# Moving the matmul operands of a one-core trunk kernel to fixed places modulo 512 bytes

## The chip, the cores and the metric

The kernel runs on one core of a Trainium2 chip. The metric is the device time in microseconds (us) of one execution, the median of three runs. The engines are called PE (TensorE, the matmul engine; PEld is its loading of weights), DVE (VectorE), ACT (ScalarE), POOL (GpSimd) and SP (SyncE, which here issues DMAs). A matmul holds one operand in the array, the stationary one, and streams the other through it, the moving one; the next stationary operand is loaded while the present moving one streams.

## The reference, cut to what matters

One layer for 256 tokens of 2048 features: `h = rmsnorm(x)`, then `proj = h @ w_in` (2048 features to 18,448 columns), which is cut into the inputs of three branches. A gated convolution of 31 taps with a layernorm, ending in `@ w_conv_out`; a gated linear attention of four heads with decays, ending in `@ w_gla_out`; a cross attention of four heads into 256 memory tokens, `rmsnorm(mem) @ w_mem_kv`, ending in `@ w_mem_out`. Three sigmoid gates weigh the branches, and `x + y @ w_out` is normalized at the end. All in float32. Nearly all the arithmetic is in the products of the 256 tokens with the weight matrices.

## The kernel before, in words

**Products.** Each float32 operand is split in two parts of 12 significant bits, `hi` and `lo`, and each product is three matmuls (`mm3`, lines 158 to 160): hi by hi, hi by lo, lo by hi. Work is done in groups of 512 output columns and 2048 input features, which are 16 tiles of 128. There are two kinds of groups:

- `group_t` puts output features on partitions. Stationary are 128 columns of the weights, moving are the 256 tokens of the activations: 16 tiles x 4 x 3 = 192 matmuls of 256 columns. There are 19 such groups, called by their output tiles: ca0 to ca3 and cb0 to cb3 (convolution), q0, q1, k0, k1, mk, mq, mz, and cz0 to cz3.
- `group_n` puts tokens on partitions. Stationary are 128 tokens, moving are the 512 columns of the weights: 16 tiles x 2 x 3 = 96 matmuls of 512 columns. On the normalized x (tiles `xh` and `xl`) these are v1 to v3, gm0 to gm3, gz0 to gz3, go0 to go3 and gc0 to gc3, 19 in all, and va and vb with 264 columns. On other operands these are mv, yo, yc, out and the short ym.

**Weights.** `chunk` streams two tiles of 128 features at a time from HBM by a DMA on SP's queue into `raw` (4 buffers), ACT copies them to `hi` (line 140) and DVE subtracts to `lo` (line 141), 5 buffers each. These three have a higher priority in the scheduler, so that they run ahead of their use.

**Side work.** Norms, taps of the convolution (`conv_taps`, 480 instructions on DVE, line 359), the scores of the linear attention and the rest are generators that `tick` advances between the chunks; their small matmuls go between those of a group. Their tiles come from rings: `t2` (2048 bytes a partition, 8 buffers), `t1`, `u`, and `b4` (4096 bytes, 19 buffers). The scheduler lays the order of each engine down when the kernel is built.

**Places in SBUF.** Tiles follow each other in a partition in the order in which they are asked for, each padded to 32 bytes. In the program of the kernel before, `xh` and `xl` start at 384 modulo 512 bytes, and `raw`, `hi`, `lo` and all `b4` tiles at 448. Within a tile, 128 columns are 512 bytes, 256 are 1024 and 512 are 2048. So in the groups on `xh` and `xl` weights lie 64 bytes after x modulo 512, and in the groups whose activations are `b4` tiles they lie at the same place. The latter are ca0, cb0, q0, k0 (x not yet normalized), mk and mv (memory), ym, yo, yc and out. In va and vb the second tile of a chunk lies another 32 bytes later, since 264 columns are 1056 bytes.

Of the kernel before, what the change touches and what calls it, by code (L numbers as in the profile page):

```python
# [16 lines left out]
P = 128  # L17
# [16 lines left out]
NB4, NB2, NB1, NRAW, NHL = 19, 8, 8, 4, 5  # L34
NU, LAG, HELD, XWAIT = 2, 2, 12, 4
SPARE = 1.2
AHEAD = 400
# [12 lines left out]
# columns of the packed per-feature vectors  # L50
# [5 lines left out]
def trunk_kernel(ctx, tc, streamed, xt, memt, x, weights, w_alpha2, vecs, taps, b_gate, b_conv_out,  # L56
# [26 lines left out]
    # ---- side work: generators that are advanced between the chunks of weights. They yield how much  # L83
    # work they gave the vector engine, or ("wait", n) to go on n chunks later. ----
# [5 lines left out]
    def start(gen, rank=1):  # L90
        """Tasks of a lower rank go first."""
        task = [gen, 0, rank]
        at = len(Side.queue)
        while at and Side.queue[at - 1][2] > rank:
            at -= 1
        Side.queue.insert(at, task)
        return task
# [28 lines left out]
    def chunk(w, k, a, cols, name, spare=False):  # L126
        """Rows of a tiles of 128 features from tile k on, cols: (first, count) side by side. The weights
        lie in memory in the order in which they are asked for."""
        b = sum(n for _, n in cols)
        at = sum(P * a * sum(n for _, n in cols) for _, _, a, cols in streamed)  # L130
        streamed.append((w, k, a, cols))
        raw = wp.tile([P, a, b], F32, name=f"raw_{name}", tag="raw", bufs=NRAW)
        if spare:
            hi, lo = b4([P, a, b], f"hi_{name}", F32R), b4([P, a, b], f"lo_{name}", F32R)
        else:
            hi = wp.tile([P, a, b], F32R, name=f"hi_{name}", tag="hi", bufs=NHL)
            lo = wp.tile([P, a, b], F32R, name=f"lo_{name}", tag="lo", bufs=NHL)
        with tc.high_priority(offset=AHEAD):
            nc.sync.dma_start(raw, weights[at:at + P * a * b].rearrange("(p k c) -> p k c", p=P, k=a))
            nc.scalar.copy(hi, raw)  # L140
            nc.vector.tensor_sub(lo, raw, hi.bitcast(F32))  # L141
        return hi, lo

    def chunks(w, cols, nk, acts, name, first=CK, spare=False):
        if not isinstance(cols, list):
            cols = [(cols, GC)]
        k = 0
        while k < nk:
            ck = min(CK, first) if k < 2 * first else CK
            hi, lo = chunk(w, k, ck, cols, f"{name}_{k}", spare and k + ck > nk - HELD and k < nk - 8)  # L150
            ops = [acts(k + kk) for kk in range(ck)]
            for kk in range(ck):
                yield k + kk, hi[:, kk, :], lo[:, kk, :], *ops[kk]
            k += ck
            tick()
# [6 lines left out]
    def group_t(w, c0, acts, nk, name, first=CK):  # L162
        """Output features on partitions: two tiles of [128, 2, tokens]."""
        pss = [mm_tile(f"pt_{name}_{j}") for j in range(2)]
        for k, hi, lo, ah, al in chunks(w, c0, nk, acts, name, first):
            for n in range(4):
                cols = slice(n * P, (n + 1) * P)
                mm3(pss[n // 2][:, (n % 2) * T:(n % 2 + 1) * T], hi[:, cols], lo[:, cols], ah, al,
                    k == 0 and n % 2 == 0, k == nk - 1)
        return [p.rearrange("p (a b) -> p a b", a=2) for p in pss]  # L170

    def group_n(w, c0, acts, nk, name):
        """Tokens on partitions: one tile of [128, 512], or of the columns, per token tile."""
# [28 lines left out]
    def token_bcast(col, r, name):  # L202
        """[tokens, 1] per token tile -> r, [128, tokens], the same row on each partition."""
# [8 lines left out]
    def feat_sum(src, name):  # L212
        """Sum over partitions of [128, tokens] -> PSUM [tokens, 1] per token tile."""
# [6 lines left out]
    def square_sum(part, src, name, squared=False):  # L220
        """part (or None) + the sum of squares over the 4 feature tiles of src."""
# [19 lines left out]
    tap = const.tile([P, KT, TAPS], F32, name="tap")  # L241
    mhalf = const.tile([P, 2], F32, name="mhalf")
    nc.gpsimd.memset(mhalf, -0.5)
    reset = const.tile([P, 2 * T], F32, name="reset")
    nc.gpsimd.memset(reset, 1.0)
    nc.gpsimd.memset(reset[:, 0:2 * T:CHUNK], 0.0)
    msk = const.tile([P, len(LEVELS), P], U8, name="msk")

# [1 line left out]
    def raw_operand(src, v0, name, keep):  # L250
        """Loads and splits as it is asked for: the operands, the loaded tiles or their squares."""
# [36 lines left out]
    mrb = const.tile([P, T], F32, name="mrb")  # L288
# [40 lines left out]
    def conv_group(g, acts, rb=None):  # L329
        pa = group_t("w_in", C_A + g * GC, acts, KT, f"ca{g}", CK if rb is None else 1)  # L330
        if g == 0:
            load_constants()
        pb = group_t("w_in", C_B + g * GC, acts, KT, f"cb{g}")
# [14 lines left out]
        return start(conv_taps(g, u), rank=2)  # L348

    def conv_taps(g, u):  # L350
        cg = b4([P, 4, T], f"conv{g}")
        conv.append(cg)
        for i in range(4):
            c = 4 * g + i
            acc = cg[:, i, :]
            nc.vector.tensor_scalar(acc, u[:, i, 0:T], tap[:, c, 0:1], vec[:, V_DB + c:V_DB + c + 1],
                                    op0=ALU.mult, op1=ALU.add)
            for j in range(1, TAPS):
                nc.vector.scalar_tensor_tensor(acc, u[:, i, j:j + T], tap[:, c, j:j + 1], acc,  # L359
                                               op0=ALU.mult, op1=ALU.add)  # L360
                yield 0.4
# [37 lines left out]
    def silu_psum(pz, name):  # L399
        """silu of a PSUM tile."""  # L400
# [8 lines left out]
    cum = []  # L409

    def decay(alr):
        """alr: per token tile the low-rank inputs, in columns 0 and 64 on the upper, 32 on the lower bits."""
# [16 lines left out]
        for i in range(2):  # L429
# [13 lines left out]
            # log_sigmoid(z) = min(z, 0) - ln(1 + exp(-|z|)); sums inside chunks of TAU * log_a  # L443
# [7 lines left out]
            for j in range(2):  # L451
                nc.vector.tensor_tensor_scan(cm[:, 2 * j:2 * j + 2, :].rearrange("p a b -> p (a b)"), reset,
                                             zb[:, 2 * j * T:2 * (j + 1) * T], 0.0, ALU.mult, ALU.add)
# [3 lines left out]
    def load_constants():  # L457
        nc.sync.dma_start(idents, ident_in)
        nc.sync.dma_start(tap, taps)
# [9 lines left out]
    def gla_head(h, q, k, v):  # L469
        """q, k: [128, 2, tokens] of the head, q scaled; v: per token tile [128, 512]."""  # L470
# [5 lines left out]
        # Scores are made as [key, query] for the two token tiles at once. The second tile has its keys  # L476
        # in reverse order, so that in each block its lower half lies where the first has its upper one.
# [13 lines left out]
        # the diagonal, where nothing decays, and pairs of neighbours, where only the query does  # L491
# [33 lines left out]
        # key in the lower and query in the upper half of a block of 2 L tokens: both decays  # L525
        # are taken to the end of the lower half, so that no exponent is positive
# [23 lines left out]
        # key in the first, query in the second half of the sequence  # L550
# [30 lines left out]
        # o = scores @ v, and its rmsnorm  # L581
# [36 lines left out]
    def v_group(h, q, k):  # L618
# [5 lines left out]
        else:  # L624
            # together with the low-rank inputs of the decays
# [98 lines left out]
    def gated_gla():  # L724
        """The normalized o times silu(z), transposed, times the gain of the norm, split."""
# [139 lines left out]
    fss = const.tile([P, NT, 4], F32, name="fss")  # L865
    def residual(po, n, t):
        """Adds x; the mean of the squares goes to fss, the gain of the final norm to res."""
# [12 lines left out]
    fs3 = const.tile([P, NT], F32, name="fs3")  # L880
# [21 lines left out]
    # the last columns: the second token tile ends HELD feature tiles after the first  # L902
# [60 lines left out]
```

## Time and profile before

| | |
|---|---|
| time, median of 3 runs | 1247.44 us (1246.75 to 1247.57) |
| span of the profiled execution | 1246.8 us |
| mean granted clock of TensorE | 0.999 |
| busy: PE, PEld, DVE, ACT, POOL | 1231.0, 1093.9, 964.0, 591.8, 18.6 us |
| instructions: PE, DVE, ACT | 7338, 1502, 711 |
| read from HBM | 235.06 MB, 190 GB/s over the span |

The profiled execution has no time of its own beside its span; the span is 0.6 us under the median of the runs and within their range. Busy is the time in which an engine has an instruction at work. Matmuls overlap, and their ends are modelled, so a matmul's own length says little; what the stream costs is read from the distance between the starts of consecutive matmuls.

### The profile page before, as it was taken

To read this page: it belongs to the slowest core of one execution; us is meant where nothing else is said; L and a number is where in the kernel's file an instruction comes from. 1 tells how busy PE (TensorE), PEld (TensorE's weight loads), DVE (VectorE), ACT (ScalarE), POOL (GpSimd) and SP (SyncE) were. 2 spreads that over 40 slices of the span, in tenths; PEclk is the share of its full clock that TensorE was granted. 3 is DMA by queue.
4 is the path that set the end of the run, shared out by engine and by line. 5 is a ranking of instruction groups with operands and counts; after the bars stand their busy time and mean duration, and the time that the engine had idled before them with its cause. 6 is when DMAs were issued, how large, how long until landed. Compare 5 with 4: busy or idle time off the path is not lost.

```text
span 1246.8 us, 18825 instructions
## 1 busy us (share of the span) xinstructions
PE 1231.0 (99%) x7338; PEld 1093.9 (88%) x7338; DVE 964.0 (77%) x1502; ACT 591.8 (47%) x711; POOL 18.6 (1%) x29
## 2 busy tenths in 40 slices
PE   7999999999999999999999999999999999999997
PEld 7999899988998998889988888888999888888885
DVE  7999999699999667999699979964565554655553
ACT  7534676446553454444445445544354444444442
POOL 0000000000020000000000000000000000000000
PEclk9999999999999999999999999999999999999999
DMA  7565745446545445665465555565555655567562
GB/s 272 186 191 170 236 153 195 155 161 221 188 165 193 159 152 183 205 204 193 161 218 171 200 201 171 179 228 194 195 183 190 202 202 195 205 227 268 187 215 71
DMA packets 71672, 238.37 MB, mean 191 GB/s; under 512 B 7792, under 2 KB 12144, under 8 KB 71584
## 3 DMA queue, kind: packets, MB, share of 16 engines
q1 hardware_dynamic: 71440, 237.13, 56.6%
q8 instruction: 57, 0.93, 0.3%
q14 instruction: 31, 0.25, 0.1%
q10 hardware_dynamic: 144, 0.05, 0.0%
HBM read 235.06 MB, written 2.10 MB: 190 GB/s over the span
## 4 chain that ended last, share of the span: by engine, by line
PE 97%; DMA 1%; DVE 1%; issue 0%; SPq 0%; ACT 0%; POOLq 0%; DVEq 0%; POOL 0%
PE pt_cb L158 2%; PE pt_cz L158 2%; PE pt_cb L159 2%; PE pt_cb L160 2%; PE pt_cz L159 2%; PE pt_cz L160 2%; PE pn_gc L159 2%; PE pn_gm L159 2%; PE pn_gz L158 2%; PE pn_go L159 2%; PE pn_go L158 2%; PE pn_gm L158 2%; PE pn_gz L159 2%; PE pn_yo L158 2%; PE pn_go L160 2%; PE pn_gc L160 2%
## 5 line engine op out<-in xcount | busy, mean ns | idle before, releaser
L359 DVE SCALAR_TENSOR_TENSOR conv<-u,tap,conv 128x256 f32<-128x256 f32 x480 | 207.3, 474 | 0.0
L158 PE MATMUL pt_ca<-xh,hi_ca 128*128 128x256 f32 x256 | 72.7, 289 | 6.1 <-ACT xh L187 5.1
L159 PE MATMUL pt_ca<-xl,hi_ca 128*128 128x256 f32 x256 | 73.5, 288 | 0.2
L160 PE MATMUL pt_ca<-xh,lo_ca 128*128 128x256 f32 x256 | 72.7, 287 | 0.9 <-DVE lo_ca L141 0.9
L158 PE MATMUL pt_cb<-xh,hi_cb 128*128 128x256 f32 x256 | 72.4, 283 | 0.0
L141 DVE TENSOR_TENSOR lo_yc<-raw_yc,hi_yc 128x1024 fp32r<-128x1024 f32 x32 | 39.2, 1225 | 42.9 <-ACT hi_yc L140 42.9
L160 PE MATMUL pt_cz<-xh,lo_cz 128*128 128x256 f32 x256 | 71.9, 281 | 0.0
L158 PE MATMUL pt_cz<-xh,hi_cz 128*128 128x256 f32 x256 | 71.9, 281 | 0.0
L159 PE MATMUL pt_cz<-xl,hi_cz 128*128 128x256 f32 x256 | 71.9, 281 | 0.0
L160 PE MATMUL pt_cb<-xh,lo_cb 128*128 128x256 f32 x256 | 71.8, 282 | 0.0
L159 PE MATMUL pt_cb<-xl,hi_cb 128*128 128x256 f32 x256 | 71.8, 281 | 0.0
L141 DVE TENSOR_TENSOR lo_cz<-raw_cz,hi_cz 128x1024 fp32r<-128x1024 f32 x32 | 39.2, 1224 | 35.7 <-ACT hi_cz L140 35.7
L141 DVE TENSOR_TENSOR lo_gc<-raw_gc,hi_gc 128x1024 fp32r<-128x1024 f32 x32 | 39.1, 1223 | 34.2 <-ACT hi_gc L140 34.2
L141 DVE TENSOR_TENSOR lo_out<-raw_out,hi_out 128x1024 fp32r<-128x1024 f32 x32 | 39.0, 1224 | 31.5 <-ACT hi_out L140 31.2
L140 ACT CAST hi_gc<-raw_gc 128x1024 fp32r<-128x1024 f32 x32 | 33.6, 1052 | 50.3 <-PE pn_yc L160 24.9
L140 ACT CAST hi_yc<-raw_yc 128x1024 fp32r<-128x1024 f32 x32 | 33.7, 1053 | 49.5 <-PE pn_gc L160 33.4
L140 ACT CAST hi_yo<-raw_yo 128x1024 fp32r<-128x1024 f32 x32 | 33.6, 1051 | 46.7 <-PE pn_go L160 23.4
L141 DVE TENSOR_TENSOR lo_yo<-raw_yo,hi_yo 128x1024 fp32r<-128x1024 f32 x32 | 38.8, 1221 | 21.6 <-ACT hi_yo L140 21.6
L158 PEld LDWEIGHTS pt_ca<-xh,hi_ca 128*128 128x128 f32 x256 | 49.5, 196 | 6.4 <-ACT xh L187 5.1
L140 ACT CAST hi_gm<-raw_gm 128x1024 fp32r<-128x1024 f32 x32 | 33.6, 1050 | 45.2 <-PE pn_gm L160 24.6
L140 ACT CAST hi_go<-raw_go 128x1024 fp32r<-128x1024 f32 x32 | 33.7, 1052 | 44.6 <-PE pn_yo L160 24.6
L140 ACT CAST hi_cz<-raw_cz 128x1024 fp32r<-128x1024 f32 x32 | 33.6, 1050 | 44.3 <-PE pt_cz L159 36.0
(352 smaller groups left out, 4108.9 us busy)
## 6 DMA issues: line engine op xcount, KB each, us to landing
raw_cb<-in_weights SPq DMA_DIRECT2D x32, 512.0 KB, 3.5
raw_gm<-in_weights SPq DMA_DIRECT2D x32, 512.0 KB, 3.2
raw_gz<-in_weights SPq DMA_DIRECT2D x32, 512.0 KB, 3.3
raw_go<-in_weights SPq DMA_DIRECT2D x32, 512.0 KB, 3.6
raw_yo<-in_weights SPq DMA_DIRECT2D x32, 512.0 KB, 3.2
raw_cz<-in_weights SPq DMA_DIRECT2D x32, 512.0 KB, 3.2
raw_gc<-in_weights SPq DMA_DIRECT2D x32, 512.0 KB, 3.2
raw_yc<-in_weights SPq DMA_DIRECT2D x32, 512.0 KB, 3.2
```

What stands on the lines that cost most here:

```text
L140: nc.scalar.copy(hi, raw)
L141: nc.vector.tensor_sub(lo, raw, hi.bitcast(F32))
L158: nc.tensor.matmul(o, lhsT=ah, rhs=bh, start=first, stop=False, skip_group_check=True)
L159: nc.tensor.matmul(o, lhsT=ah, rhs=bl, start=False, stop=False, skip_group_check=True)
L160: nc.tensor.matmul(o, lhsT=al, rhs=bh, start=False, stop=last, skip_group_check=True)
L359: nc.vector.scalar_tensor_tensor(acc, u[:, i, j:j + T], tap[:, c, j:j + 1], acc, op0=ALU.mult, op1=ALU.add)
```

## The change

- Constants are rearranged: `tap` (1984 bytes a partition) goes; each convolution group loads its own 496 bytes into a ring of two, by a DMA on SP's queue between its two products. `reset` is half as long, so that the scan of `decay` is 8 instructions of 256 columns in place of 4 of 512. `fss` and `fs3` are made earlier. `mrb` is the same tile as `xrb`. `t2` has 7 buffers.
- By the sizes of the tiles, `xh` then starts at 23424 - 1984 - 1024 + 64 = 20480 bytes, which is 0 modulo 512, and `raw`, `hi`, `lo` and `b4` start at 0 too. `hi` and `lo` tiles are 4608 bytes, nine times 512.
- For `group_t` alone the view of the weights starts 64 bytes into `hi` and `lo` (LINE is 16 elements), and in chunks 0 and 4 of a group (KICK) the second tile starts at 128 modulo 512. In ca0, whose first two chunks hold one tile each, these are tiles 0, 1 and 9, in all others tiles 1 and 9. Activations lie at 0.
- For `group_n` weights and activations lie at 0, also in va and vb, whose second tile now starts 2048 bytes after the first.

Comments are taken out; nothing else of the order in which the program is written changes.

```diff
-NB4, NB2, NB1, NRAW, NHL = 19, 8, 8, 4, 5
+NB4, NB2, NB1, NRAW, NHL = 19, 7, 8, 4, 5
+LINE, HLW = 16, CK * GC + P
+KICK = (0, 4)
...
+    def parts(a, b, name, spare, at):
+        both = []
+        for part in ("hi", "lo"):
+            if spare:
+                t = b4([P, a, b], f"{part}_{name}", F32R)
+                both.append([t, [t[:, j, :] for j in range(a)]])
+                continue
+            t = wp.tile([P, HLW], F32R, name=f"{part}_{name}", tag=part, bufs=NHL)
+            step, first = GC, 0
+            if at:
+                first = LINE * at[0]
+                step = GC + LINE * (at[-1] - at[0])
+            v = t[:, first:first + a * step].rearrange("p (k c) -> p k c", k=a)[:, :, 0:b]
+            both.append([v, [v[:, j, :] for j in range(a)]])
+        return both
...
-        if spare:
-            hi, lo = b4([P, a, b], f"hi_{name}", F32R), b4([P, a, b], f"lo_{name}", F32R)
-        else:
-            hi = wp.tile([P, a, b], F32R, name=f"hi_{name}", tag="hi", bufs=NHL)
-            lo = wp.tile([P, a, b], F32R, name=f"lo_{name}", tag="lo", bufs=NHL)
+        (hi, his), (lo, los) = parts(a, b, name, spare, lines)
...
+            lines = None
+            if shifted:
+                lines = [1] * (ck - 1) + [2 if k // CK in KICK else 1]
+            hi, lo = chunk(w, k, ck, cols, f"{name}_{k}", spare and k + ck > nk - HELD and k < nk - 8, lines)
...
-        for k, hi, lo, ah, al in chunks(w, c0, nk, acts, name, first):
+        for k, hi, lo, ah, al in chunks(w, c0, nk, acts, name, first, shifted=True):
...
-    tap = const.tile([P, KT, TAPS], F32, name="tap")
...
-    reset = const.tile([P, 2 * T], F32, name="reset")
+    reset = const.tile([P, T], F32, name="reset")
...
+    fss = const.tile([P, NT, 4], F32, name="fss")
+    fs3 = const.tile([P, NT], F32, name="fs3")
...
-    mrb = const.tile([P, T], F32, name="mrb")
+    mrb = xrb
...
+        tap = tp.tile([P, 4, TAPS], F32, name=f"tap{g}", tag="tap")
+        nc.sync.dma_start(tap, taps[:, 4 * g:4 * g + 4, :])
         pb = group_t("w_in", C_B + g * GC, acts, KT, f"cb{g}")
...
-                nc.vector.tensor_tensor_scan(cm[:, 2 * j:2 * j + 2, :].rearrange("p a b -> p (a b)"), reset,
-                                             zb[:, 2 * j * T:2 * (j + 1) * T], 0.0, ALU.mult, ALU.add)
+                for f in range(2 * j, 2 * j + 2):
+                    nc.vector.tensor_tensor_scan(cm[:, f, :], reset, zb[:, f * T:(f + 1) * T], 0.0,
+                                                 ALU.mult, ALU.add)
```

## Rows read from the trace of the kernel before

**Rows 1.** The page: busy time by engine, and the chain that ended last.
```profile
PE 1231.0 (99%) x7338; PEld 1093.9 (88%) x7338; DVE 964.0 (77%) x1502; ACT 591.8 (47%) x711; POOL 18.6 (1%) x29
...
PE 97%; DMA 1%; DVE 1%; issue 0%; SPq 0%; ACT 0%; POOLq 0%; DVEq 0%; POOL 0%
```

**Rows 2.** All waits of PE: for whom, us in total, times, longest.
```profile
PE pt_ca L158 <- ACT xh L187: 5.1, 1, 5.1
PE pt_ca L158 <- ACT hi_ca L140: 1.0, 1, 1.0
PE pt_ca L160 <- DVE lo_ca L141: 0.9, 1, 0.9
```

**Rows 3.** Timeline of PE, first matmuls of groups: start, length.
```profile
59.20 0.28 PE L158 MATMUL pt_q<-xh,hi_q 128*128 128x256 f32 x1
...
105.28 0.28 PE L158 MATMUL pn_va<-hi_va,xh 128*128 128x264 f32 x1
...
881.99 0.28 PE L158 MATMUL pt_cz<-xh,hi_cz 128*128 128x256 f32 x1
...
972.44 0.40 PE L158 MATMUL pn_gc<-hi_gc,xh 128*128 128x512 f32 x1
...
994.43 0.39 PE L158 MATMUL pn_yc<-hi_yc,uh 128*128 128x512 f32 x1
...
1016.19 0.39 PE L158 MATMUL pn_gc<-hi_gc,xh 128*128 128x512 f32 x1
```

**Rows 4.** Timeline of PE inside group ca2, around small matmuls of side work.
```profile
302.97 0.28 PE L158 MATMUL pt_ca<-xh,hi_ca 128*128 128x256 f32 x1
...
312.83 0.28 PE L158 MATMUL pt_ca<-xh,hi_ca 128*128 128x256 f32 x1
...
313.17 0.60 PE L518 MATMUL pl<-d 128*128 128x128 f32 x4
...
313.97 0.28 PE L158 MATMUL pt_ca<-xh,hi_ca 128*128 128x256 f32 x1
...
323.16 0.28 PE L158 MATMUL pt_ca<-xh,hi_ca 128*128 128x256 f32 x1
```

**Rows 5.** Line 158 in both stretches of ca2: count, min/median/max ns, first and last start.
```profile
L158 PE MATMUL pt_ca<-xh,hi_ca x30: 276/276/276, 303.0 to 312.8; 128*128 128x256 f32 x30
...
L158 PE MATMUL pt_ca<-xh,hi_ca x27: 281/281/281, 314.0 to 323.2; 128*128 128x256 f32 x27
```

**Rows 6.** Group va: a later matmul in the timeline, and line 158's count up to it.
```profile
113.29 0.28 PE L158 MATMUL pn_va<-hi_va,xh 128*128 128x264 f32 x1
...
L158 PE MATMUL pn_va<-hi_va,xh x23: 279/284/288, 105.3 to 113.3; 128*128 128x264 f32 x23
```

**Rows 7.** Windows of the first 349 us: busy us of each engine (instructions), PEclk, DMA.
```profile
105.00:152.00 47.00, 47.00 (x303) 42.86 (x302) 46.61 (x89) 25.78 (x35) 0.00 (x0) 1.00 0.72 223
...
246.00:349.00 103.00, 103.00 (x687) 93.66 (x686) 99.07 (x188) 56.67 (x76) 1.23 (x2) 1.00 0.56 191
sum 318.00, PE 318.00 PEld 303.08 DVE 297.32 ACT 173.98 POOL 4.47; mean PE 79.50 PEld 75.77 DVE 74.33 ACT 43.50 POOL 1.12
```

**Rows 8.** Timelines of DVE and PE: the first chunk of v1, split and first used.
```profile
126.18 1.22 DVE L141 TENSOR_TENSOR lo_v<-raw_v,hi_v 128x1024 fp32r<-128x1024 f32 x1
...
129.10 0.40 PE L159 MATMUL pn_v<-lo_v,xh 128*128 128x512 f32 x1
```

**Rows 9.** The taps of the convolution, line 359: min/median/max ns, first and last start.
```profile
L359 DVE SCALAR_TENSOR_TENSOR conv<-u,tap,conv x480: 457/475/490, 69.6 to 732.9; 128x256 f32<-128x256 f32 x160
```

**Rows 10.** Timeline of POOL: memsets of u2 and u3, which wait for taps' ends.
```profile
214.48 0.20 POOL L335 MEMSET u<- 128x120 f32 x1 [172.65 <-DVE conv L359]
...
415.79 0.20 POOL L335 MEMSET u<- 128x120 f32 x1 [0.40 <-DVE conv L359]
```

**Rows 11.** Waits of DVE: scores for PE's small matmuls on t2 tiles.
```profile
DVE sT L520 <- PE pl L518: 1.9, 3, 0.9
```

**Rows 12.** The page: the cast of line 140 for cz.
```profile
L140 ACT CAST hi_cz<-raw_cz 128x1024 fp32r<-128x1024 f32 x32 | 33.6, 1050 | 44.3 <-PE pt_cz L159 36.0
```

More of the change, by code (lines that the diff above doesn't have):

```diff
@@ L123, in finish, with chunk @@
                 advance(task)
-    def chunk(w, k, a, cols, name, spare=False):
+    def parts(a, b, name, spare, at):
[13 more added lines that the diff above has]
+        return both
+    def chunk(w, k, a, cols, name, spare=False, lines=None):
         b = sum(n for _, n in cols)
@@ L141, in chunk, with chunks @@
             nc.vector.tensor_sub(lo, raw, hi.bitcast(F32))
-        return hi, lo
-    def chunks(w, cols, nk, acts, name, first=CK, spare=False):
+        return his, los
+    def chunks(w, cols, nk, acts, name, first=CK, spare=False, shifted=False):
         if not isinstance(cols, list):
@@ L149, in chunks @@
             ck = min(CK, first) if k < 2 * first else CK
-            hi, lo = chunk(w, k, ck, cols, f"{name}_{k}", spare and k + ck > nk - HELD and k < nk - 8)
+            lines = None
+            if shifted:
+                lines = [1] * (ck - 1) + [2 if k // CK in KICK else 1]
+            hi, lo = chunk(w, k, ck, cols, f"{name}_{k}", spare and k + ck > nk - HELD and k < nk - 8, lines)
             ops = [acts(k + kk) for kk in range(ck)]
             for kk in range(ck):
-                yield k + kk, hi[:, kk, :], lo[:, kk, :], *ops[kk]
+                yield k + kk, hi[kk], lo[kk], *ops[kk]
             k += ck
@@ L240, in trunk_kernel @@
     ident, flip = idents[:, 0, :], idents[:, 1, :]
-    tap = const.tile([P, KT, TAPS], F32, name="tap")
     mhalf = const.tile([P, 2], F32, name="mhalf")
     nc.gpsimd.memset(mhalf, -0.5)
-    reset = const.tile([P, 2 * T], F32, name="reset")
+    reset = const.tile([P, T], F32, name="reset")
     nc.gpsimd.memset(reset, 1.0)
-    nc.gpsimd.memset(reset[:, 0:2 * T:CHUNK], 0.0)
+    nc.gpsimd.memset(reset[:, 0:T:CHUNK], 0.0)
     msk = const.tile([P, len(LEVELS), P], U8, name="msk")
+    fss = const.tile([P, NT, 4], F32, name="fss")
+    fs3 = const.tile([P, NT], F32, name="fs3")
     def raw_operand(src, v0, name, keep):
@@ L347, in conv_group, with conv_taps @@
                 nc.vector.tensor_mul(ua, ua, rbb)
-        return start(conv_taps(g, u), rank=2)
-    def conv_taps(g, u):
+        return start(conv_taps(g, u, tap), rank=2)
+    def conv_taps(g, u, tap):
         cg = b4([P, 4, T], f"conv{g}")
@@ L355, in conv_taps @@
             acc = cg[:, i, :]
-            nc.vector.tensor_scalar(acc, u[:, i, 0:T], tap[:, c, 0:1], vec[:, V_DB + c:V_DB + c + 1],
+            nc.vector.tensor_scalar(acc, u[:, i, 0:T], tap[:, i, 0:1], vec[:, V_DB + c:V_DB + c + 1],
                                     op0=ALU.mult, op1=ALU.add)
             for j in range(1, TAPS):
-                nc.vector.scalar_tensor_tensor(acc, u[:, i, j:j + T], tap[:, c, j:j + 1], acc,
+                nc.vector.scalar_tensor_tensor(acc, u[:, i, j:j + T], tap[:, i, j:j + 1], acc,
                                                op0=ALU.mult, op1=ALU.add)
@@ L458, in load_constants @@
         nc.sync.dma_start(idents, ident_in)
-        nc.sync.dma_start(tap, taps)
     def load_masks():
@@ L864, in trunk_kernel @@
         nc.sync.dma_start(fg[i], final_g[i * (D // 2):(i + 1) * (D // 2)].unsqueeze(0).to_broadcast([P, D // 2]))
-    fss = const.tile([P, NT, 4], F32, name="fss")
     def residual(po, n, t):
@@ L879, in trunk_kernel @@
             residual(po[t], n, t)
-    fs3 = const.tile([P, NT], F32, name="fs3")
     for t in range(NT):
```

## The prediction

> **What bounds the kernel now.** I read the page first. PE is busy nearly all the span, and 97% of the chain that ended last is PE [rows 1]. Then PE's waits: there are three in the whole execution, 7.0 us together, all in the first group [rows 2]. So from about 31 us on PE never stands still until the last rows are normalized, and no DMA or other engine is late: whatever this change gives or takes must come out of the distance between matmuls, or by making another engine late that now is not.
>
> So the next view is PE's timeline, from which I take distances between starts, over whole groups where nothing interrupts. The reader is to see that matmuls of one shape, all at a granted clock of 1.00 (the 2.4 GHz level) [rows 7], don't have one distance:
>
> - q0 and k0, 256 columns, weights and activations at the same place modulo 512: 384 matmuls from 59.20 to 105.28 us [rows 3], 46.08 / 384 = 120.0 ns.
> - cz0 to cz3, 256 columns, weights 64 bytes later: 768 matmuls from 881.99 to 972.44 [rows 3], 117.8 ns.
> - ca2, also 64 bytes later: 30 matmuls of line 158, one in three, from 302.97 to 312.83, so 9.86 / 87 = 113.3 ns; then four small matmuls of the scores come in between, and 27 of line 158 from 313.97 to 323.16 give 9.19 / 78 = 117.8 ns [rows 4, 5].
> - gc0, 512 columns, x 64 bytes before the weights: 96 from 972.44 to 994.43, 229.1 ns. Right behind it yc0, both at the same place: 96 up to 1016.19, 226.7 ns [rows 3].
> - va, 264 columns, places apart by 64 and 96 bytes: line 158 from 105.28 to 113.29, 23 times, so 8.01 / 66 = 121.4 ns [rows 3, 6].
>
> Two things follow. Relative place matters: 226.7 is twice 113.3, the same per column, and nothing here is quicker, so I take 113.3 ns per 256 columns as the floor and the rest as what place costs. And at 64 bytes with 256 columns there are **two steady paces**, the short one of 113.3 ns and the long one of 117.8, with the same tiles at the same places. Scanning the timeline of all groups, a pace holds as long as the stream is unbroken, over tiles, chunks and groups; after a break by side work it is now the one, now the other. Groups entered from 512-column ones without a break (cz, ca3) run at the long pace. At the same place, 256 columns are always at 120.0.
>
> **The change part by part.**
>
> *512 columns to the same place.* 19 groups of 96 go from 229.1 to 226.7: 1824 x 2.39 ns = 4.4 us. The new relative place is that of yc, measured, so this is the surest term. va and vb: the floor is 113.3 x 264 / 256 = 116.9 ns; 192 x 4.5 = 0.9 us at most, nothing at least; I take 0.6, as all other same-place streams of moving weights sit at the floor. Together **5.0**.
>
> *256 columns, the five groups now at 120.0* (ca0, cb0, q0, k0, mk) go to 64 bytes. At the floor four of them give 192 x 6.7 = 1.28 each; ca0, where PE waits for loads, half: 5.7 us. At the long pace it is 192 x 2.2 x 4.5 = 1.9.
>
> *256 columns, the 14 groups on xh and xl* stay at 64 bytes. Eight keep the long pace throughout (ca1, ca3, cb3, mz, cz0 to cz3), six change pace at breaks (cb1, q1, k1, ca2, cb2, mq); I count those as half long. At the short pace everywhere this is 8 x 0.85 + 6 x 0.43 = 9.4 us, but only if the two odd tiles of 16 bring the stream over. Nothing in the trace lies at 128 bytes, so the price of such a tile is bounded by the nearest rows, 113.3 to 120.0. Twelve matmuls at another relative place are a break of the kind that shifts loads against streams, without the gap of a foreign matmul. Since a break by side work comes at any moment and this one always at the same point of the same pattern, I expect the same pace after each, and take the short one: the long one is where unbroken streams already are. Ceiling with the five: 15.1 us. I take a fifth of the 3648 matmuls as still at the long pace (the odd tiles, tile 0 before the first, side work's breaks until the next odd tile, which in ca1 to mz come several to a group): 730 x 4.4 ns = 3.2 us. That leaves **11.9**.
>
> *DVE.* A quicker PE needs its weights earlier, and ACT and DVE must make them. In 31 to 349 us DVE is busy 297.3 of 318; in 105 to 152 it has 0.4 us left, and in 246 to 349, 3.9 [rows 7]. The smallest lead after the start is at v1: its first `lo` ends at 127.40 and is used at 129.10 [rows 8], 1.7 us. By then PE would be some 4 us ahead of its old times (cb0, q0, k0, half of ca0, va and vb, at four fifths). DVE gains part of it back, since some of its idle time before is waiting for buffers that PE then frees earlier. I charge **1.5 us**; the ends are 0 and all that is gained before 349 us (a rival, below).
>
> *Costed at nothing.* The scan in 8 pieces adds four DVE instructions for the same columns; a whole tap of 256 columns is 475 ns [rows 9], so this is 1.9 us of DVE at the very most, and I leave it inside the 1.5. The cast and the subtraction write the same 1024 columns, in two runs in the odd chunks; ACT has half its time free, a cast is 1050 ns and ACT waits longer for buffers than it works on cz [rows 12]. The places of DVE's operands move too; the 480 taps, over all channels and both `u` buffers, lie between 457 and 490 ns [rows 9], so place is worth 16 us of DVE at the very most, after 349 us hidden by its idle time, before it part of the DVE rival. The four loads of `tap`: those of g = 2 and 3 must wait on SP's queue for the taps of g = 0 and 1, with the weights' DMAs behind them. These end at 214.5 and 415.8 [rows 10]; ca2 starts at 302 and ca3 at 568, and SP's raw loads wait for the same DVE queue, so the order holds. `mrb` is written long after the last use of `xrb`. `t2` with seven: the last merge needs six tiles for a block and one for the next bias, seven; the scores hold three or four. If it is short, DVE waits for PE's small matmuls as it does three times now, 0.6 us each [rows 11]; 24 such tiles at that price are 15 us of DVE, the far end; I take nothing.
>
> *Sum.* 5.0 + 11.9 - 1.5 = 15.4 us off a span of 1246.8, which is 0.6 under the median of the runs: 1247.4 - 15.4 = **1232.0 us**.
>
> The Trainium skill ("TensorE: Matmul & The Clock Gate", Step-by-step: what each phase is for) says PE has two independent read ports, one for the moving operand and one for loading weights. By that rule the relative place of the two is worth nothing and the sum is 0. The trace doesn't agree: 120.0 against 113.3 ns for the same shape [rows 3 to 5]. I keep it as a rival, since my distances are also ordered by group and time.
>
> **The rivals.**
>
> - *The odd tiles don't bring the short pace.* For it: an unbroken stream keeps its pace, and the break in ca2 ends in the long one [rows 4, 5]. Against: the same rows show that a break can change it. Then 5.0 + 1.9 - 1.0 (456 odd matmuls at up to 120) = 5.9: 1241.5.
> - *DVE takes over.* All gained before 349 us is lost to late `lo` tiles: of the sum, 1.3 from v1 to v3, va and vb, and four fifths of 7.4 from the ten 256-column groups, 7.2, in place of 1.5. Left 9.7: 1237.7. For it, 47 us with 0.4 us of DVE to spare; against, 20.7 us of idle DVE over the stretch [rows 7].
> - *Place is not the cause.* If q0 and cz differ by what runs beside them and not by place, nothing moves: 1247.4. Against: gc0 and yc0 follow each other without a gap, of one shape, at 229.1 and 226.7 [rows 3].
> - *Slower: the odd tiles lock the stream at 120.0.* The pace of q0 and k0 is as steady as the others, and nothing in the trace shows which one a tile at 128 leads to. Then the 14 groups lose 8 x 192 x 2.2 + 6 x 192 x 4.5 = 8.5 us, the five nothing, and the 512-column ones still give 5.0: 1251. The mean of 256 columns is now 113.3 + 15.1 us / 3648 = 117.5 ns; it decides for slower from 118.9 on, where 5.0 us are eaten.
>
> **How the numbers follow.** Short pace 0.60, odd tiles without effect 0.17, DVE takes over 0.10, place not the cause 0.06, locked at 120.0 0.07. The prediction is the first, 1232.0; alone it spans from 1227 (ceiling 15.1 + 5.2 and no DVE loss) to 1237 (half of the matmuls left at the long pace: 5.0 + 7.0 - 1.5 = 10.5). To hold eight in ten it must take in the DVE rival and the one without effect: 1226 to 1242. Faster by over 0.2% (2.5 us, about what a measurement of this kernel can tell from no change) holds in the first three cases, 0.87; same 0.06; slower 0.07.
>
> **What would show it.** In the timeline after: q0 and k0 at 113 to 118 and not 120.0; cz, the cleanest stretch, 768 matmuls at 113.3 to 114.5 after tile 1 of cz0, or still 117.8; gc at 226.7 like yc; va near 117. PE's waits should stay at some 7 us, with at most 2 us new ones on `lo` tiles around v1 and cb1. DVE's `lo` leads before 349 us should shrink. The prediction is wrong if cz stays at 117.8 or goes to 120, if the first 349 us keep their length while cz shrinks, or if PE shows waits for `t2` users or raw loads that were not there.

## The result and the profile after

| | before | after |
|---|---|---|
| time, median of 4 runs each, on one chip | 1247.51 us (1246.75 to 1247.72) | 1232.57 us (1232.3 to 1233.35) |
| ratio, 95% interval | | 0.988 (0.9866 to 0.9894) |
| span of the profiled execution | 1246.8 us | 1231.5 us |
| mean granted clock of TensorE | 0.999 | 0.996 |

The change makes the kernel 14.9 us quicker; the forecast was 1232.0. The page first: busy time by engine, and the chain that ended last.

```profile
PE 1215.1 (99%) x7338; PEld 1082.0 (88%) x7338; DVE 963.2 (78%) x1506; ACT 592.0 (48%) x711; POOL 19.7 (2%) x29
...
PE 98%; DMA 1%; DVE 0%; ACT 0%; SPq 0%; issue 0%; POOLq 0%; DVEq 0%; POOL 0%
```

The reader is to see that PE's busy time went from 1231.0 us [rows 1] to 1215.1, so by 15.9 us, close to the 15.3 us of span, with the same 7338 matmuls. PEld, the loading of weights, fell by 11.9 us; DVE, ACT and POOL stay within 1.1 us. Then all waits of PE (for whom, us in total, times, longest):

```profile
PE pt_ca L177 <- ACT xh L206: 4.6, 1, 4.6
PE pt_ca L179 <- DVE lo_ca L157: 2.5, 1, 2.5
PE pt_ca L177 <- ACT hi_ca L156: 0.3, 1, 0.3
```

There are three as before and all in ca0, 7.4 us where it was 7.0 [rows 2]. None went and none came at another place, but the one for `lo_ca` grew from 0.9 to 2.5 us while the other two shrank. It is 2.1 to 2.8 us in every kernel below with the new layout and 1.1 in experiment 7 with the old one; why, no run shows. ca0 as a whole, from its first matmul to that of cb0, takes 24.6 to 26.2 us over all executions, longest in the kernel before, so no price of it shows. The gain is in the distances between matmuls. Line 177 of the changed kernel is line 158 of the one before. The timeline of PE, first matmuls of the groups of [rows 3] and the later one of va that answers to [rows 6] (start us, length):

```profile
57.23 0.28 PE L177 MATMUL pt_q<-xh,hi_q 128*128 128x256 f32 x1
...
101.00 0.29 PE L177 MATMUL pn_va<-hi_va,xh 128*128 128x264 f32 x1
...
108.93 0.28 PE L177 MATMUL pn_va<-hi_va,xh 128*128 128x264 f32 x1
...
870.10 0.28 PE L177 MATMUL pt_cz<-xh,hi_cz 128*128 128x256 f32 x1
...
957.68 0.40 PE L177 MATMUL pn_gc<-hi_gc,xh 128*128 128x512 f32 x1
...
979.47 0.39 PE L177 MATMUL pn_yc<-hi_yc,uh 128*128 128x512 f32 x1
...
1001.23 0.39 PE L177 MATMUL pn_gc<-hi_gc,xh 128*128 128x512 f32 x1
```

- q0 and k0: (101.00 - 57.23) / 384 = 114.0 ns, before 120.0.
- cz0 to cz3: (957.68 - 870.10) / 768 = 114.0 ns, before 117.8.
- gc0: (979.47 - 957.68) / 96 = 227.0 ns, before 229.1; yc0, right behind it: 226.7 as before.
- va: (108.93 - 101.00) / 66 = 120.2 ns, before 121.4.

One row by line shows the same in less room, and stands for each kernel below: the count, the min/median/max length of one matmul in ns, and the first and last start. Line 177 in q0, k0 and cz after the change:

```profile
L177 PE MATMUL pt_q<-xh,hi_q x64: 276/276/285, 57.2 to 78.8; 128*128 128x256 f32 x64
...
L177 PE MATMUL pt_k<-xh,hi_k x64: 276/276/285, 79.1 to 100.7; 128*128 128x256 f32 x64
...
L177 PE MATMUL pt_cz<-xh,hi_cz x256: 276/276/285, 870.1 to 957.3; 128*128 128x256 f32 x128
```

Line 177 is one matmul in three, so from the first to the last of 256 there are 3 x 255 = 765 distances: 87.2 us / 765 = 114.0 ns. The modelled length goes with the pace: 276 ns was the length in the short stretch of ca2 and 281 in the long one [rows 5]. A median of 276 says that most of the matmuls run at the short pace, a maximum of 285 that some don't. They are the 12 to 24 matmuls at and behind each odd tile.

The windows of DVE's tightest stretches, moved to where those groups now lie (busy us and instructions of PE, PEld, DVE, ACT, POOL, then PEclk, DMA share, GB/s):

```profile
101.00:147.00 46.00, 46.00 (x299) 42.08 (x298) 45.94 (x87) 25.42 (x35) 0.00 (x0) 1.00 0.70 223
...
240.00:343.00 103.00, 103.00 (x691) 94.01 (x691) 99.34 (x189) 56.93 (x77) 1.23 (x2) 1.00 0.56 190
```

DVE has 0.1 us left of 46 where it had 0.4 of 47, and 3.7 of 103 where it had 3.9 [rows 7]. The first chunk of v1, split by DVE and first used by PE, from the timelines of the two engines:

```profile
122.09 1.22 DVE L157 TENSOR_TENSOR lo_v<-raw_v,hi_v 128x1024 fp32r<-128x1024 f32 x1
```

```profile
124.53 0.39 PE L178 MATMUL pn_v<-lo_v,xh 128*128 128x512 f32 x1
```

It ends at 123.31 and is used at 124.53: the lead is 1.2 us, where it was 1.7 [rows 8]. In this execution it was not used up; experiments 7 and 8 show how much it varies.

**Where the 15.3 us of span came from.** I summed over the whole trace by how much each distance between starts exceeds the floor, 113.3 ns per 256 columns (116.9 for 264, 226.7 for 512), leaving out those of more than 16 ns above it, which stand next to small matmuls of side work or in PE's waits. The kernel before has 21.9 us of such excess, 16.2 in 256-column groups and 5.8 in the others; the changed one has 6.6, 5.1 and 1.5. So the 256-column groups gave 11.1 us and the others 4.25, together 15.4; what was left out grew by 0.3 (ca0), and some 0.1 lies ahead of the first matmul and behind the last.

### The profile page after: what moved, and what is told of

Same layout as the page of the kernel before. It is cut to its first block, busy times and chain, and to the rows that moved or that the text cites. A ratio compares the mean times of both kernels' runs of the same rounds, so it can differ in the third digit from the quotient of the medians.

```text
span 1231.5 us, 18833 instructions
## 1 busy us (share of the span) xinstructions
PE 1215.1 (99%) x7338; PEld 1082.0 (88%) x7338; DVE 963.2 (78%) x1506; ACT 592.0 (48%) x711; POOL 19.7 (2%) x29
## 4 chain that ended last, share of the span: by engine, by line
PE 98%; DMA 1%; DVE 0%; ACT 0%; SPq 0%; issue 0%; POOLq 0%; DVEq 0%; POOL 0%
PE pt_cb L177 2%; PE pt_cb L178 2%; PE pt_cz L178 2%; PE pt_cb L179 2%; PE pn_yo L177 2%; PE pt_cz L177 2%; PE pn_gm L177 2%; PE pn_gz L177 2%; PE pn_gz L178 2%; PE pn_gm L179 2%; PE pn_out L179 2%; PE pn_yo L179 2%; PE pt_cz L179 2%; PE pn_gc L177 2%; PE pn_out L178 2%; PE pn_gc L178 2%
## 5 line engine op out<-in xcount | busy, mean ns | idle before, releaser
L381 DVE SCALAR_TENSOR_TENSOR conv<-u,tap,conv 128x256 f32<-128x256 f32 x480 | 211.7, 490 | 0.0
L156 ACT CAST hi_out<-raw_out 128x1024 fp32r<-128x1024 f32 x32 | 33.5, 1054 | 44.3 <-PE pn_out L179 29.6
L156 ACT CAST hi_gz<-raw_gz 128x1024 fp32r<-128x1024 f32 x32 | 33.8, 1055 | 42.7 <-PE pn_gz L179 28.9
```

## The experiments

All start from the changed kernel. "Excess" is the sum above, of the 256-column groups alone.

**1. No odd tiles.**

```diff
-KICK = (0, 4)
+KICK = ()
```

> The changed kernel with all 16 tiles of a 256-column group at 64 bytes, none at 128. If the odd tiles are what brings the short pace: cz0 to cz3, ca3 and cb3 at 117.8 ns, as before the change, and a span 7 to 11 us longer than the changed kernel's, 1239 to 1243. If it is the new layout as such (x and all else at 0 modulo 512), or anything else of the change: cz stays at 114.0 and the span within 1 us of 1231.5.

Measured: 1239.38 us (1238.62 to 1241.82), ratio 0.9933 (0.9916 to 0.9949). cz, line 177:

```profile
L177 PE MATMUL pt_cz<-xh,hi_cz x256: 280/281/282, 875.7 to 965.8; 128*128 128x256 f32 x128
```

90.1 / 765 = 117.8 ns and no matmul of 276 among them. q0, k0, ca3 and cb3 are at 117.8 too, the excess is 14.0 us and the 512-column groups are as in the changed kernel. So the two odd tiles of sixteen are what brings the short pace; by the medians they are worth 6.8 us of the 14.9. The profiled execution was the slowest of the four (1241.82 us, the others 1238.62 to 1239.83), so its excess goes with a span 8.5 us over that of the changed kernel; what the quicker three did otherwise no trace shows.

**2. All 256-column weights at x's place.**

```diff
-                lines = [1] * (ck - 1) + [2 if k // CK in KICK else 1]
+                lines = [0] * ck
```

> The changed kernel with the weights of 256-column groups at 0, where x is. If the relative place sets the pace: 120.0 ns in all undisturbed 256-column groups, cz too, 3648 x some 5 ns = 17 to 19 us more than the changed kernel, so 1249 to 1251 and a little slower than the kernel before; 512 columns stay at 226.7. If q0 and k0 were at 120.0 before the change for what ran beside them: cz at 118 or less and 1240 or less.

Measured: 1250.92 us (1249.73 to 1251.2), ratio 1.0025 (1.0014 to 1.0035), slower than before.

```profile
L177 PE MATMUL pt_cz<-xh,hi_cz x256: 278/283/284, 883.3 to 975.1; 128*128 128x256 f32 x128
...
L177 PE MATMUL pn_gc<-hi_gc,xh x32: 389/389/396, 975.4 to 996.5; 128*128 128x512 f32 x32
```

cz is at 91.8 / 765 = 120.0 ns, the pace of q0 in the kernel before. These are the same tiles, the same order and the same neighbours as in experiment 1, 64 bytes apart in the weights alone: relative place by itself makes 117.8 or 120.0. What suits 512 columns is the worst of these for 256.

**3. 512-column weights 64 bytes behind x again.** Of the groups on `xh` and `xl` only, va and vb among them.

```diff
                 lines = [1] * (ck - 1) + [2 if k // CK in KICK else 1]
+            elif acts is X:
+                lines = [1] * ck
```

> The changed kernel with the weights of the 512-column groups on xh and xl (and va, vb) 64 bytes after x, as before the change; 256 columns as changed. If relative place costs them 2.4 ns each: gc at 229.1 and yc at 226.7, some 4.3 us more, 1235.8. If the 512-column gain came from the absolute place: no difference.

Measured: 1237.8 us (1237.58 to 1238.05), ratio 0.9922 (0.9907 to 0.9937). Line 179 is the first matmul of `mm3` here:

```profile
L179 PE MATMUL pn_gc<-hi_gc,xh x32: 387/388/390, 961.0 to 982.3; 128*128 128x512 f32 x32
```

From the first matmul of gc0 to that of yc0 it takes 22.0 us for 96, 229 ns, with yc0 at 226.9 (226.7 in the changed kernel); va is at 121.0. The excess of the groups that are not 256 wide goes from 1.5 to 6.5 us, that of the 256-column ones stays at 5.0. The span is 4.3 us longer, since what is left out of the sum happened to be 0.9 us less, nearly all in ca0. That is the 512-column term of the prediction, taken back.

**4. Whole groups at other places.** Without odd tiles in six undisturbed groups, each `lines = [at] * ck` in steps of 64 bytes: ca3 320, cb3 384, cz0 128, cz1 192, cz2 256, cz3 448 bytes behind x.

> The changed kernel with all tiles of six undisturbed groups at one other place each, no odd tiles in them: ca3 320, cb3 384, cz0 128, cz1 192, cz2 256, cz3 448 bytes after x. The theory of two paces has nothing to say on which of these has the short one; each is between 113.3 and 120.0. If one is at 113.3 from its first tile on, odd tiles are not needed there; if 128 were at 113.3, the odd tiles would be the short pace themselves rather than a push to it. The span moves by at most 6 x 192 x 6 ns = 7 us.

Measured in a single run: 1238.17 us. Line 179 in the six groups, in this order:

```profile
L179 PE MATMUL pt_ca<-xh,hi_ca x64: 280/281/282, 559.0 to 581.3; 128*128 128x256 f32 x64
...
L179 PE MATMUL pt_cb<-xh,hi_cb x64: 278/281/286, 581.6 to 604.1; 128*128 128x256 f32 x64
...
L179 PE MATMUL pt_cz<-xh,hi_cz x64: 280/282/288, 871.2 to 893.9; 128*128 128x256 f32 x64
...
L179 PE MATMUL pt_cz<-xh,hi_cz x64: 278/279/283, 894.3 to 916.5; 128*128 128x256 f32 x64
...
L179 PE MATMUL pt_cz<-xh,hi_cz x64: 280/284/288, 916.9 to 939.6; 128*128 128x256 f32 x64
...
L179 PE MATMUL pt_cz<-xh,hi_cz x64: 278/279/280, 939.9 to 962.2; 128*128 128x256 f32 x64
```

From first matmul to first matmul of the next group, divided by 192: 117.8, 118.7, 120.0, 117.8, 120.0 and 117.8 ns. No place brought the short pace by itself, entered as it was here (ca3 and cz0 behind a group of 512 columns, the others behind the one listed before), and 128, where the odd tiles lie, is at 120.0 when a whole group lies there. So the odd tile does not carry the short pace; it only throws the stream onto it. What a whole group at one of these places would do behind a short stream was not tried.

**5. Which throw works.** All tiles at 64, and in the first chunk of a group one tile elsewhere: ca3 none, cb3 tile 0 at 0, cz0 tile 1 at 192, cz1 tile 1 at 256, cz2 tile 1 at 128, cz3 none.

```diff
+PUSH = {"ca3": None, "cb3": [0, 1], "cz0": [1, 3], "cz1": [1, 4], "cz2": [1, 2], "cz3": None}
...
+                if name in PUSH:
+                    lines = PUSH[name] if k == 0 and PUSH[name] else [1] * ck
```

> The changed kernel with other odd tiles in the undisturbed groups, one to a group in its first chunk: none in ca3, the first tile at 0 in cb3, the second at 192 in cz0, at 256 in cz1, at 128 in cz2, none in cz3. ca3 and cz0 are entered at the long pace. If any other place pushes the stream over: cb3 at 113.3 behind its first tile, cz0 too, and cz1 to cz3 stay there. If only 128 does: 117.8 in all up to tile 1 of cz2, and 113.3 from there through cz3, which has no odd tile. If a push must be repeated to hold: cz3 back at 117.8.

Measured in a single run: 1234.98 us. Line 180, in this order:

```profile
L180 PE MATMUL pt_ca<-xh,hi_ca x64: 281/281/281, 559.2 to 581.4; 128*128 128x256 f32 x64
...
L180 PE MATMUL pt_cb<-xh,hi_cb x64: 281/281/283, 581.8 to 604.1; 128*128 128x256 f32 x64
...
L180 PE MATMUL pt_cz<-xh,hi_cz x64: 276/276/281, 871.2 to 892.7; 128*128 128x256 f32 x64
...
L180 PE MATMUL pt_cz<-xh,hi_cz x64: 276/281/283, 893.1 to 915.3; 128*128 128x256 f32 x64
...
L180 PE MATMUL pt_cz<-xh,hi_cz x64: 276/276/285, 915.7 to 937.2; 128*128 128x256 f32 x64
...
L180 PE MATMUL pt_cz<-xh,hi_cz x64: 276/276/276, 937.6 to 959.0; 128*128 128x256 f32 x64
```

The medians tell the story. ca3 is long throughout. The tile at 0 in cb3 is slow itself (283 ns) and throws nothing. The tile at 192 takes cz0 from long to short. The tile at 256 throws cz1 from short back to long. The one at 128 brings cz2 to short again, and cz3 stays there for 192 matmuls with no odd tile at all: the minimum and the maximum are 276. A stream keeps its pace, and a single tile can move it either way, by its place. Each throw is seen once here, in one execution. Those by 128 and 192 come back in other kernels (the changed one, experiments 10 to 12); those by 0 and 256 were not repeated, and the tile at 0 was the first of its chunk where the others were the second.

**6. Odd tiles only where a stream needs one.** In a short stream an odd tile at 128 costs 0.06 us (an excess of 0.12 us in cz1, which has two). I dropped them from groups entered at the short pace and put others behind the breaks that side work makes.

```diff
-KICK = (0, 4)
+KICKS = {"ca0": (0, 4), "cb0": (2,), "ca1": (0,), "cb1": (4, 6), "q1": (2, 4), "k1": (5,), "ca2": (0, 4), "cb2": (0, 3),
+         "mk": (2, 5), "mq": (2, 5), "mz": (1, 4), "ca3": (0,), "cz0": (0,)}
```

> The changed kernel with odd tiles at 128 only where a pace is to be changed: one in the first chunk of ca1, ca3 and cz0, none in q0, k0, cb3, cz1 to cz3, and one behind those breaks by side work that leave two or more tiles in the groups cb0 to mz. An odd tile costs some 0.06 us, a long tile 0.053 us. By the two paces: 0.8 us for 14 odd tiles less in undisturbed groups, and 0.5 to 1.2 us in the others, so 1 to 2 us under the changed kernel. If the pace is lost between groups without a push: up to 4 us over it.

Measured: 1233.7 us (1231.51 to 1234.42), ratio 0.9885 (0.9869 to 0.9902): nothing gained beside the changed kernel on the same chip (experiment 8), and an excess of 6.0 us. cb3 and cz1 to cz3 are at 113.3 as hoped, but the one odd tile of cb0 fell on a tile that side work interrupts, did not throw, and q0 and k0 then ran at 117.8, with an excess of 0.85 us each.

**7. Everything but the places.** All other edits (the loads of `tap`, the scan in eight, seven `t2`, `mrb`) stay, while no weights are shifted and padding puts `xh` at 384 and the weights at 448, as in the kernel before.

```diff
+    const.tile([P, 96], F32, name="pad0")
...
+    const.tile([P, 16], F32, name="pad1")
...
-            if shifted:
-                lines = [1] * (ck - 1) + [2 if k // CK in KICK else 1]
```

> All edits but the places: the changed kernel with 384 bytes put in ahead of xh and 64 ahead of raw, and no offsets, so that xh and xl lie at 384 and raw, hi, lo and the b4 tiles at 448 modulo 512, as before the change; tap loads, halved scan, shared xrb and seven t2 buffers as changed. If all of the gain is place: the time of the kernel before within 1 us, cz at 117.8, q0 at 120.0, gc at 229.1. If the other edits have a share: below 1246; if seven t2 buffers or the tap loads cost: above 1249.

Measured: 1247.66 us (1247.11 to 1248.35), ratio 1.0001 (0.9992 to 1.001). Line 175, from two stretches:

```profile
L175 PE MATMUL pt_cz<-xh,hi_cz x256: 281/281/281, 880.4 to 970.5; 128*128 128x256 f32 x128
...
L175 PE MATMUL pn_gc<-hi_gc,xh x32: 392/392/398, 970.8 to 992.1; 128*128 128x512 f32 x32
```

117.8 ns in cz, 229.1 in gc0, 120.0 in q0. (The second tile of a chunk of va and vb lies at 64 here and not at 96: 120.9 ns in place of 121.6, 0.1 us in all.) The lead at v1 is 1.1 us, so between two executions with the old places it differs by 0.6. All of the gain is place, and the edits that make room for it cost nothing that shows.

**8. The changed kernel again**, beside 6 and 7.

> The changed kernel itself once more, to be compared with the one before last on the same chip: 1232.6 within 1 us.

Measured: 1233.42 us (1232.57 to 1233.91), ratio 0.9886 (0.9872 to 0.9901). The excess is 5.5 us where it was 5.1, all of the difference in ca0 and cb0; every later 256-column group is within 0.01 us of its first profile. So the paces behind cb0 come back the same, and sums that differ by 0.5 us do not tell two kernels apart.

This execution shows less room for DVE than the first profile. The first `lo` of v1 and its first use:

```profile
122.88 1.22 DVE L157 TENSOR_TENSOR lo_v<-raw_v,hi_v 128x1024 fp32r<-128x1024 f32 x1
```

```profile
124.46 0.39 PE L178 MATMUL pn_v<-lo_v,xh 128*128 128x512 f32 x1
```

The lead is 0.35 us. The second `lo` of q0, the first matmul that reads it, and the one behind that:

```profile
57.38 1.23 DVE L157 TENSOR_TENSOR lo_q<-raw_q,hi_q 128x1024 fp32r<-128x1024 f32 x1
```

```profile
58.67 0.39 PE L179 MATMUL pt_q<-xh,lo_q 128*128 128x256 f32 x1
58.89 0.28 PE L177 MATMUL pt_q<-xh,hi_q 128*128 128x256 f32 x1
```

The tile ends at 58.61 and is read 0.06 us later, with 0.22 us to the next matmul: PE loses 0.1 us there, too little for a row among its waits. In the first profile this lead was 1.1 us, and with the old places 2.1 (the kernel before and experiment 7).

**9. Other chosen tiles.** As 6, with cb0's odd tile one chunk later, and those of k1 and of mk, mq and mz moved off the breaks or dropped.

```diff
-KICKS = {"ca0": (0, 4), "cb0": (2,), "ca1": (0,), "cb1": (4, 6), "q1": (2, 4), "k1": (5,), "ca2": (0, 4), "cb2": (0, 3),
-         "mk": (2, 5), "mq": (2, 5), "mz": (1, 4), "ca3": (0,), "cz0": (0,)}
+KICKS = {"ca0": (0, 4), "cb0": (3,), "ca1": (0,), "cb1": (4, 6), "q1": (2, 4), "ca2": (0, 4), "cb2": (0, 3),
+         "mk": (2, 6), "mq": (5,), "mz": (1,), "ca3": (0,), "cz0": (0,)}
```

> The kernel with chosen pushes, with those that failed there moved at least one tile away from a break by side work (cb0 to its fourth chunk, mk to its seventh) and those without effect left out (k1, one each in mq and mz). If a push needs a settled stream before it: q0 and k0 at 113.3 without an odd tile, all of the 256-column groups some 3.8 us over the floor of 113.3 where the changed kernel has 5.1 and the chosen pushes had 6.0; 1.0 to 1.5 us under the changed kernel, about what a measurement can tell. If pushes fail at random: no better than the changed kernel.

Measured: 1231.72 us (1231.28 to 1232.24), ratio 0.9873 (0.9857 to 0.989), an excess of 3.5 us; k0 is at 113.3 with no odd tile. That is 0.9 and 1.7 us under the two medians of the changed kernel, with intervals that overlap. PE's waits have a new row:

```profile
PE pt_q L180 <- DVE lo_q L158: 0.7, 1, 0.7
```

It stands at the matmul of q0 shown in experiment 8. Behind ca0 no kernel above has a wait of PE for DVE among its rows but experiment 4 (0.2 us, at the same place). The stretch is one that the prediction's DVE rival is about.

**10. Odd tiles at 192.** Experiment 5 left open what a tile at 192 costs a stream that is already short.

```diff
-                lines = [1] * (ck - 1) + [2 if k // CK in KICK else 1]
+                lines = [1] * (ck - 1) + [3 if k // CK in KICK else 1]
```

> The changed kernel with its odd tiles at 192 in place of 128. In the look at other pushes a tile at 192 brought the long pace over within its own length at 117.8, a tile at 128 runs at 118 to 120. If 192 also leaves a stream that is already at the short pace there: cz at or under 114.0, and as fast as the changed kernel or 0.5 us faster. If it throws such a stream out, as 256 did: cz alternates between the paces, half of the push is lost, 4 to 5 us slower.

Measured in a single run: 1232.45 us. In a short stream it costs nothing: q0, k0, cb3 and cz1 to cz3 are at 113.3 ns, with two tiles at 192 in each. The excess is 4.5 us, since several of these tiles fell where side work breaks the stream (cb1 stays long from its first break to its end).

**11 and 12. 192 in every chunk, and in every second.** If such a tile is free in a short stream, more of them are more chances for a broken one.

```diff
-                lines = [1] * (ck - 1) + [3 if k // CK in KICK else 1]
+                lines = [1] * (ck - 1) + [3]
```

> The last tile of every chunk of weights lies 192 bytes later than x, all others 64; no tile lies at 128. Theory: a tile at 192 is a push that throws a long stream onto the short pace and costs a short stream nothing, so eight tiles are eight chances for each group; then cz and cb3 stand at 113.3 to 114.0 ns, the groups that side work breaks come back to the short pace within two tiles, the sum of 256-column matmuls above the floor is 2.5 to 4 us (5.05 in the changed kernel), and the time 1230.5 to 1232. Rival: 192 has a pace of its own (a whole group at 192 stood at 117.8 ns) and half of the tiles there pull the mean up: 115 to 118 ns in cz, an excess of 8 to 14 us, and 1235 to 1240.

```diff
-KICK = (0, 4)
+KICK = (0, 2, 4, 6)
```

> The last tile of chunks 0, 2, 4 and 6 lies 192 bytes later than x, all others 64. Theory: four chances for each group at no cost in a short stream: cz at 113.3 to 114.2 ns, an excess of 3 to 4.5 us over the floor, and 1231 to 1232.5. Rival (192 holds the long pace while it lasts): 114.5 to 116 ns in cz and 1233 to 1237, between the changed kernel and the one with 192 in every chunk.

Measured: with every chunk 1230.87 us (1230.35 to 1231.76), ratio 0.9871 (0.9854 to 0.9887); with every second 1230.91 (1230.78 to 1231.24), 0.987 (0.9855 to 0.9884). Line 177 with 192 in every chunk:

```profile
L177 PE MATMUL pt_q<-xh,hi_q x64: 276/276/276, 56.4 to 77.8; 128*128 128x256 f32 x64
...
L177 PE MATMUL pt_k<-xh,hi_k x64: 276/276/276, 78.2 to 99.6; 128*128 128x256 f32 x64
...
L177 PE MATMUL pt_cz<-xh,hi_cz x256: 276/276/281, 867.8 to 954.6; 128*128 128x256 f32 x128
```

Half of the tiles lie at 192, where a whole group is at 117.8, and not one matmul of q0 or k0 leaves the short pace. The excess is 3.06 us (3.64 with every second). The rival, in which the tiles at 192 pull the mean up, is out. PE's waits in the same execution:

```profile
PE pt_ca L177 <- ACT xh L206: 4.7, 1, 4.7
PE pt_ca L179 <- DVE lo_ca L157: 2.5, 1, 2.5
```

and DVE from 100 to 146 us, before the end of v1:

```profile
100.00:146.00 46.00, 46.00 (x299) 42.08 (x299) 45.49 (x86) 25.39 (x35) 0.00 (x0) 1.00 0.72 218
```

The wait of experiment 9 is not there, with a PE that is ahead of it. Against the changed kernel these two are 1.7 us shorter in the medians, 0.1% by the ratios to before (0.987 against 0.988), and the intervals overlap: the profiles show 2.0 and 1.4 us less excess than the changed kernel's first one, the times alone don't settle it.

## Why the prediction was right

**What bounds the kernel.** It held: the time moved through the distances between matmuls alone, with three waits before and three after, all in ca0, in the executions profiled for the result.

**512 columns, 5.0 forecast, 4.25 measured.** Of this the 19 groups gave 3.85 and not 4.4; gc0 went to 227.0 and not fully to 226.7, and some that side work interrupts keep a little. Groups whose places did not change gave 0.1. va and vb gave 0.3 and not 0.6: they stay at 120.2, which is not the floor of 116.9. The reason given, that moving weights at the same place sit at the floor, is not true for 264 columns, or 116.9 is not their floor; no run tells which. Experiment 3 takes the term back at 5.0 us of excess.

**The five groups at 120.0, between 1.9 and 5.7.** They gave 4.5: ca0 0.8, cb0 1.0, q0 and k0 1.15 each, mk 0.4. mk is the low one: behind a break in its fifth tile it runs at 117.8 ns until its second odd tile brings it over, and a break in the tile behind that throws it back for the last five tiles.

**The 14 groups on x.** They gave 6.65 of a ceiling put at 9.4. Their excess before was 10.2: cb1 and mq, counted as half long, were by this sum nearly all long (0.83 and 0.77 of 0.85 us). With the five this is 11.1, forecast 11.9, since 5.1 us are left and not 3.2. The step "a fifth of the matmuls still at the long pace" was the one mis-sized: in cb1 to mz a break by side work throws the stream to the long pace, and it stays there until the next odd tile that works, which those right at a break often don't. q1 and k1 even became slower, with 0.61 and 0.57 us of excess where it was 0.48 and 0.39. In the undisturbed groups it was about right: a fifth of the matmuls at the long pace would be 0.17 us, and 0.12 to 0.18 are left in each.

**The odd tiles.** The rival without effect had 1241.5; experiment 1 is that case, at 1239.4. The expectation that each odd tile leaves "the same pace after each" and that it is the short one held in every undisturbed group. The argument for it was weaker than the outcome: "a break of the kind that shifts loads against streams" would fit any odd place, but experiment 5 shows that the place decides: 256 threw to the long pace, 128 and 192 throw to the short one, and 0 did nothing. Nothing in the trace before could have told 128 from 256, so that the place chosen was one that works was luck.

**Locked at 120.0.** It was the right price for another kernel: 1251 forecast, and 1250.9 in experiment 2, where all tiles lie at x's place. It is also what a whole group at 128 does (120.0, experiment 4). Two tiles at 128 in sixteen don't lock the stream.

**Place is not the cause.** Out by experiments 1, 2 and 7. The Trainium skill ("TensorE: Matmul & The Clock Gate", Step-by-step: what each phase is for) gives PE two independent read ports for the moving operand and the weight load. Read as leave to choose their places freely, that doesn't hold here: the same matmuls stand at 113.3, 117.8 or 120.0 ns by relative place and by what came before.

**DVE, 1.5 forecast, at most 0.1 measured behind ca0.** No wait came in the first profile and one of 0.1 us in the second (experiment 8). The lead at v1, 1.7 us before and 1.2 after, does not show that leads shrank: it was 1.1 in experiment 7 with the old places and 0.35 in the repeat. The lead of q0's second `lo` does: 2.1 in both executions with the old places, 1.1 and 0.06 with the new ones. The charge was too large in its offset, "DVE gains part of it back": PE needs v1's first `lo` 4.6 us earlier than before in both executions, and DVE ends it 4.1 and 3.3 us earlier. With 192 in every chunk PE is another us ahead there and still does not wait. So the rival did not come about, but it is near, and how near differs by execution: experiment 9 has the 0.7 us, experiments 11 and 12 have nothing.

**Costed at nothing.** Together confirmed by experiment 7 (ratio 1.0001); not told apart one by one. The taps, 475 ns in the median before [rows 9], have a median of 484 in the profiled execution after.

**The base of the sum.** The forecast took a run as 0.6 us longer than its span. In every execution for which both are known it is 1.8 (1233.35 us and 1231.5 for the profile after). So the trace read before belongs to an execution about 1 us longer than the median, that after to one 0.8 us longer, and 15.3 us less span go with 14.9 less time. The terms' errors, 0.75 and 0.8 too much gain and 1.5 too much loss, nearly cancel. That the forecast came within 0.6 us of the time is luck in this; that the gain lies in the distances, by place and by the odd tiles, is what the experiments bear out.

## What to carry to other kernels

Where PE never waits, take the distance between starts of matmuls group by group, undisturbed stretches first, and compare it with the shortest one in the trace: a few per cent that a group keeps from its first matmul to its last can be the places of the two operands. Try the relative place modulo 512 bytes for each shape by itself, since the same place, the better of the two tried for 512 moving columns, was among the worst for 256. Where two paces exist at one place, look for what throws the stream from one to the other, and try many cheap throws: a few chosen ones need care to miss the breaks by side work (an excess of 6.0 us in experiment 6 and 3.5 in 9, against 3.0 and 3.6 with many in 11 and 12). These differences are at the edge of what the times can tell.

## What the runs showed of the hardware

- Start-to-start distance of 256-column matmuls by how far the weights lie behind x modulo 512, at a granted clock of 1.00: 120.0 ns at 0, 128 and 256; 117.8 at 192, 320 and 448; 118.7 at 384; at 64 either 117.8 or 113.3. The values other than at 0 and 64 are of one group each in one execution (experiment 4). For 512 columns: 226.7 at 0, 229.1 at 64.
- At 64 the two paces are held over hundreds of matmuls. A tile of twelve matmuls at 128 or 192 in a long stream leads to the short one; one at 256 led from short to long, and one at 0 changed nothing in a long stream, both seen once. In a short stream a tile at 128 costs 0.06 us, one at 192 nothing that shows.
- Small matmuls of side work throw the stream more often to the long pace: behind 19 of the 25 breaks in the kernel before that leave at least five distances to read, in groups on `xh` and `xl`, and behind 23 of 34 in experiment 1, in all groups but ca0.
- Why there are two paces, and what in the chip the place modulo 512 bytes meets, no run here shows. It also stays open whether a tile throws by its own place or by the step from one place to another, and it was not tried whether these places hold when the moving operand and not the stationary one is shifted in 256-column groups.
